# Hybrid decoder layer on one core: when the first attention loads may start, who stores two gate tiles, and how the planner counts transfers in flight

## The chip, the cores and the metric

The kernel runs on one core of a Trainium2 chip. The metric is device time in microseconds (us), as the median of several runs. Inputs and the output are float32 in device memory.

## The reference

One layer over 1040 tokens (16 learned tokens ahead of 1024) of width 1024. All four branches read the same projection z of the normalised input.

```python
h = rms_norm(h_res, pre_norm_g[i])
z = h @ w_in[i]                                    # 1024 -> 7328 columns
(pv, pg, cq, ckv, kr, mg, cu, cg, sbcx, sg, gl) = split_cols(z)
y_a = (pool_mixer(pv, ...) * silu(pg)) @ w_out_pool[i]
y_b = (mla_attention(cq, ckv, kr, ...) * silu(mg)) @ w_out_mla[i]      # 8 heads, causal
y_c = (conformer_conv(cu, ...) * silu(cg)) @ w_out_conf[i]
y_d = (short_conv(sbcx, ...) * silu(sg)) @ w_out_sc[i]
gts = sigmoid(gl + gate_bias[i])                   # four gates of 1024 channels
m = gts[0] * y_a + gts[1] * y_b + gts[2] * y_c + gts[3] * y_d
h_res = h_res + rms_norm(m @ w_o[i], post_norm_g[i])
```

In `mla_attention` a key has 64 columns of its own for each head and 32 rotary columns `k_rope` that all heads share.

## The kernel before

Float32 operands are split into a high and a low part and each product is made of three matmuls. The program has three stages, and each is planned and written out by itself.

**Projections.** Pairs of column blocks of `w_in` are loaded (`raw`), combined on VectorE (`ss`), split by ScalarE and GpSimd into operand tiles (`A`, `S`) and multiplied into the PSUM banks `pa` to `pd`. `out_gate` writes the gate tiles `th` to device memory: all by ScalarE's queue, but for the last pair (`g == 30`), which goes by GpSimd's queue. Work that needs earlier projections (convolution, norms, keys, queries, values, pool) runs beside this in four lanes. Keys go to `k` (64 rows for each head) and `kr` (32 rotary rows) in device memory.

**Attention.** The loop runs over 16 half-heads `(h, c)`, eight heads by two halves of 512 queries. `load_q` brings a query tile (`qt`, three buffers), `load_kv` a key tile and a value tile; there are two of each (`kt0`, `kt1`, `vt0`, `vt1`), used by even and by odd heads. The rotary rows of a key tile are loaded only once, since they are the same for all heads; `kt1` has them with their halves of 16 rows exchanged, as its queries do. `maxima` makes the scores once (`ps_s<-kt,qt`), takes masked maxima of the rows on VectorE (`mx`, with the mask `maskS` that GpSimd writes at the start of the stage), transposes the result (`ps_s<-ident,md`) and copies it into four further rows of `qt` (ScalarE, `qt<-ps_s`). `attend` makes scores (`ps_s<-qt,kt`), exponentials (`p`), a high part on ScalarE and a low part on GpSimd (`pt`), and the value products (`ps_o`). `head_out` divides (VectorE `op`), multiplies with the gate path (GpSimd `op<-op,smg`) and splits the result (`boM`). `refill` hands out 48 fills, six matmuls each (`ps_y<-bo,whl`, 288 in all): output projections of the three other branches, which the planner gives a low priority. Behind each fill VectorE multiplies with the gate (`th<-th,ps_y` or `m<-th,ps_y`) and, for the second and third branch, an addition follows (`m<-m,th`; for the third on VectorE).

**Output.** `ps_u<-boM,whl` is the attention's output projection; then come the product with `w_o`, the last norm and the stores.

**What sets the order.** `Plan.record` notes each operation with what it depends on and a priority. `Plan.flush` runs through estimated times, gives each engine the ready operation of highest priority that `fits`, and then writes all engines' instructions in that order. SyncE's queue (SP) issues nearly all transfers, in order, and blocks on the first one whose waits are not met. `fits` lets SP and ScalarE issue a transfer only while fewer than eight are thought to be in flight; `self.landed` holds their estimated landing times. `plan.behind()` makes what is recorded inside depend on the last matmul recorded so far.

Of the kernel before, what the change touches and what calls it, by code (L numbers as in the profile page):

```python
# [14 lines left out]

# [49 lines left out]
def f(ap):  # L65
    return ap.bitcast(F32)
# [127 lines left out]
class Plan:  # L194
# [139 lines left out]
    def flush(self):  # L334
# [26 lines left out]
        def slot(b, t):  # L361

            free = [sl for sl in b.group["slots"] if not sl["live"] and sl["after"] <= t]
            if free and (b.group["any"] or b.group["order"][b.group["next"]] is b):
                return min(free, key=lambda sl: (sl["after"], sl["i"]))

        def fits(o, t):

            if o["op"] == "dma_start" and o["eng"] != "POOL" and len(self.landed) >= 8 and self.landed[-8] > t:
                return False  # L370
            return all(slot(b, t) for b in o["bufs"] if not b.live and b.group)

        while events:
            t = events[0][0]
            while events and events[0][0] <= t:
                _, kind, i = heapq.heappop(events)
                if kind == 0:
                    o = self.ops[i]
                    bisect.insort(ready[o["eng"]], (o["prio"], o["i"]))
                elif kind == 2:  # L380
                    for b in self.ops[i]["bufs"]:
                        b.left -= 1
                        if b.left == 0 and b.group:
                            b.slot["live"], b.slot["after"] = None, t
            for e in self.free:
                if self.free[e] > t:
                    continue
                o = next((self.ops[i] for _, i in ready[e] if fits(self.ops[i], t)), None)
                if o is None:
                    if e == "PE" and self.idle and self.ops[self.idle[1]]["end"] is None:  # L390
                        order.append(self.idle[0])
                        self.free[e] = t + 160
                        heapq.heappush(events, (self.free[e], 1, 0))
                    continue
                ready[e].remove((o["prio"], o["i"]))
                for b in o["bufs"]:
                    if not b.live:
                        b.live = True
                        if b.group:
                            b.slot = slot(b, t)  # L400
                            b.slot["live"] = b
                            b.group["next"] += 1
                o["start"] = t
                if o["turns"]:
                    o["cost"] += max(0, self.port[{"DVE": "POOL", "POOL": "DVE"}[e]] - t) * 0.7
                    self.port[e] = t + o["cost"]
                self.free[e] = t + o["cost"]
                o["end"] = t + o["cost"] + self.WAKE[e]
                if o["op"] == "dma_start":
                    if self.pipe is None:  # L410
                        self.pipe = max((x["done"] for x in self.ops if x["op"] == "dma_start"
                                         and "done" in x and x["start"] <= t), default=0)
                    o["done"] = self.pipe = max(self.pipe, t) + o["bytes"]
                    land = self.pipe + o["bytes"] + 4500 + min(0, o["extra"])
                    o["end"] = land + max(0, o["extra"])
                    if o["eng"] != "POOL":
                        self.landed.append(land)
                    heapq.heappush(events, (land, 1, 0))
                for b in o["bufs"]:
                    b.last = max(b.last, o["end"])  # L420
                order.append(o)
                heapq.heappush(events, (self.free[e], 1, 0))
                heapq.heappush(events, (o["end"], 2, o["i"]))
                for u in o["users"]:
                    u["need"] -= 1
                    same = u["eng"] == e and o["op"] != "dma_start"
                    u["at"] = max(u["at"], self.free[e] if same else o["end"])
                    if not u["need"]:
                        heapq.heappush(events, (u["at"], 0, u["i"]))
# [8 lines left out]
def trunk_kernel(ctx, tc, a):  # L438
    nc = tc.nc
    plan = Plan(nc)  # L440
    PE, ACT, DVE, POOL, SP = (plan.engine(e) for e in ("PE", "ACT", "DVE", "POOL", "SP"))
# [7 lines left out]
    def ld(out, in_):  # L449
        SP.dma_start(f(out) if out.dtype == F32R else out, f(in_) if in_.dtype == F32R else in_)  # L450
# [38 lines left out]
    th_dram = [dram.tile([P, NT], F32, name=f"th{i}") for i in range(32)]  # L489
# [6 lines left out]
    kr_dram = dram.tile([32, 2, L], F32R, name="kr")  # L496
# [136 lines left out]
    def full(to, x, ps):  # L633

        if x is None:
            copy(to, ps)
        else:
            add(DVE, to, ps, x)

    def pairs_of_halves(n, each, store):  # L640

        z = {}

        def out(i, j, ps, x, tmp):
            first = i not in z
            if first:
                z[i] = up.tile([P, 2, n], F32, tag="z", bufs=2, name="z")
            m = ps.shape[0]
            each(i, z[i][:m, j], ps, x, tmp)
            if not first:  # L650
                store(i, z[i][:m])
        return out
# [11 lines left out]
    def row(t):  # L664
        return t.rearrange("p j n -> p (j n)")
# [16 lines left out]
    def out_gate(g):  # L682

        def each(i, to, ps, x, tmp):
            if x is not None:
                full(to, x, ps)
            ACT.activation(to, ps if x is None else to, AF.Tanh, scale=0.5,
                           bias=par[:, R_GB + g + i:R_GB + g + i + 1])
        return pairs_of_halves(512, each, lambda i, t: (POOL if g == 30 else ACT).dma_start(th_dram[g + i], row(t)))

# [587 lines left out]
    def load_q(h, c):  # L1280
        qt[h, c] = qk.tile([NA, 2, 512], F32R, tag="q", bufs=3, name="qt")
        ld(qt[h, c][:QK].rearrange("p s n -> p (s n)"), q_dram[c][h].rearrange("p s n -> p (s n)"))

    load_q(0, 0)
    kt = [qk.tile([NA, 2, L], F32R, name=f"kt{i}") for i in range(2)]
# [4 lines left out]
    def load_kv(h):  # L1290
        e, k_, v_ = h % 2, kt[h % 2], vt[h % 2]
        ld(k_[:64].rearrange("p s n -> p (s n)"), k_dram[h // 2][64 * e:64 * (e + 1)].rearrange("p s n -> p (s n)"))
        if h == 0:
            ld(k_[64:96], kr_dram)
        if h == 1:
            ld(k_[64:80], kr_dram[16:])
            ld(k_[80:96], kr_dram[:16])
        v = v_dram[h // 4][h % 4]
        ld(v_[:, 0:8].rearrange("p j c -> p (j c)"), v[:, 0:8].rearrange("p j c -> p (j c)"))
        ld(v_[:NM, 8], v[:NM, 8])  # L1300
# [95 lines left out]
    op, smg = {}, {}  # L1396
# [58 lines left out]
    def refill():  # L1455
        count["u"] += 1
        while count["f"] < min(48, 48 * count["u"] / (NUNIT - 2)):

            with plan.ahead(-400):
                next(fill, None)  # L1460
            count["f"] += 1
# [9 lines left out]
    def lead_to(i, n=0):  # L1471

        while lead["i"] <= min(i, len(seq) - 1) or lead["steps"] < n:
            if next(steps, "end") == "end":
                lead["steps"] = math.inf
            lead["steps"] += 1

    load_kv(0)
    load_q(*seq[1])
    lead_to(0)  # L1480
    units = 0
    for i, (h, c) in enumerate(seq):
        with plan.behind():
            if i + 2 < len(seq):
                load_q(*seq[i + 2])
            if c == 0 and h + 1 < H:
                load_kv(h + 1)
            if c == 0 and h % 2:
                smg[h] = at.tile([P, NT], F32, tag="smg", name="smg")
                ld(smg[h], z_dram[f"mg{h // 2}"])  # L1490
        for _ in attend(h, c):
            units += 1
            lead_to(-1, min(5 + units * 10 / 14, 5 * (i + 3)))
            refill()
        lead_to(i + 1)
        with plan.ahead(-300):
            if h == H - 1:
                head_out(h, c, sums_pe(h, c))
            elif c:
                for k, rb in enumerate(sums(h)):  # L1500
                    head_out(h, k, rb)
# [82 lines left out]
    for d in (0, 4, 1, 5, 2, 6, 3, 7):  # L1584
# [3 lines left out]
        for c in range(2):  # L1588
            t = th[:, 512 * c:512 * (c + 1)]
# [23 lines left out]
    def half(name, bufs=4):  # L1613
        return ep.tile([P, 512], F32, tag=name, bufs=bufs, name=name)
# [71 lines left out]
    for t in range(4):  # L1686

        parts = [slice(0, 512)] if t < 3 else [slice(0, 256), slice(256, 512)]
        g = half("g", 1) if t == 3 else a_[t]
# [45 lines left out]
```

## Time and profile before

| | us |
|---|---|
| median of 3 runs | 1018.12 (1017.72 to 1019.06) |
| the profiled execution | 1017.58 |
| its span in the profile | 1015.9 |
| TensorE busy in the span | 990.5 (98%) |
| GpSimd, VectorE, ScalarE busy | 685.6, 668.1, 455.4 |

The profiled execution has 1.68 us around its span and lies 0.54 us under the median. In the profile PE is TensorE's matmuls, PEld its weight loads, DVE VectorE, ACT ScalarE, POOL GpSimd, SPq the queue of SyncE. Names are the program's tile names; all recorded operations carry line 332, the helper that issues them, so they are told apart by tile. The first number of a row of the timeline is the start, the second the duration, and in brackets stands how long the engine was idle ahead of the row and what ended that. The stages meet at about 651 us (first attention score) and 883 us (first `ps_u`).

### The profile page before, as it was taken

To read this page: it belongs to the slowest core of one execution; us is meant where nothing else is said; L and a number is where in the kernel's file an instruction comes from. 1 tells how busy PE (TensorE), PEld (TensorE's weight loads), DVE (VectorE), ACT (ScalarE), POOL (GpSimd) and SP (SyncE) were. 2 spreads that over 40 slices of the span, in tenths; PEclk is the share of its full clock that TensorE was granted. 3 is DMA by queue.
4 is the path that set the end of the run, shared out by engine and by line. 5 is a ranking of instruction groups with operands and counts; after the bars stand their busy time and mean duration, and the time that the engine had idled before them with its cause. 6 is when DMAs were issued, how large, how long until landed. Compare 5 with 4: busy or idle time off the path is not lost.

```text
span 1015.9 us, 15303 instructions
## 1 busy us (share of the span) xinstructions
PE 990.5 (98%) x5139; PEld 831.7 (82%) x5139; DVE 668.1 (66%) x1106; ACT 455.4 (45%) x911; POOL 685.6 (67%) x640
## 2 busy tenths in 40 slices
PE   9999999999999999999999999989999999799996
PEld 9999898889888878887877888868887878588885
DVE  6754795997999499435455453255565675598747
ACT  7632234443354544444534444136556556224632
POOL 6767867766777666768776765125678876556956
PEclk9999999999999999999999999989999999899998
DMA  7278755679767856566656456877568671662634
GB/s 246 75 229 277 245 169 182 217 226 301 250 214 224 288 189 206 188 197 203 206 175 197 136 172 191 310 206 241 147 188 256 183 209 53 201 228 89 202 120 165
DMA packets 126302, 203.13 MB, mean 200 GB/s; under 512 B 19650, under 2 KB 79161, under 8 KB 124880
## 3 DMA queue, kind: packets, MB, share of 16 engines
q1 hardware_dynamic: 121600, 185.38, 58.2%
q10 hardware_dynamic: 4336, 15.73, 4.2%
q8 instruction: 40, 0.66, 0.3%
q0 software_dynamic: 288, 1.05, 0.3%
q14 instruction: 38, 0.31, 0.1%
HBM read 128.40 MB, written 73.72 MB: 199 GB/s over the span
## 4 chain that ended last, share of the span: by engine, by line
PE 91%; DVE 4%; issue 2%; DMA 1%; POOL 1%; ACT 1%; SPq 0%; DVEq 0%; POOLq 0%; ACTq 0%
PE ps_pa L332 16%; PE ps_pb L332 16%; PE ps_pc L332 15%; PE ps_o L332 10%; PE ps_y L332 8%; PE ps_s L332 7%; PE ps_pd L332 7%; PE ps_u L332 7%; PE ps_x L332 4%; DMA kt<-kr 1%; DVE x L332 1%; DVE a L332 1%; DMA x<-in_x_dram 0%; DVE ps_w L332 0%; DVE ss L332 0%
## 5 line engine op out<-in xcount | busy, mean ns | idle before, releaser
L332 PE MATMUL ps_pb<-T,S 128*128 128x512 f32 (+2 forms) x792 | 172.4, 362 | 0.8 <-DVE u L332 0.8
L332 PE MATMUL ps_pa<-B,A 128*128 128x512 f32 (+2 forms) x792 | 172.2, 362 | 0.0
L332 POOL TENSOR_TENSOR S<-ss,S 128x512 fp32r<-128x512 f32 x84 | 110.5, 1328 | 76.9 <-ACT S L332 76.7
L332 PEld LDWEIGHTS ps_pa<-B,A 128*128 128x128 f32 x792 | 134.6, 188 | 24.4 <-issue 0.5
L332 PEld LDWEIGHTS ps_pb<-T,S 128*128 128x128 f32 x792 | 133.8, 188 | 24.4 <-DVE u L332 1.2
L332 POOL TENSOR_TENSOR A<-raw,A 128x512 fp32r<-128x512 f32 x84 | 116.9, 1397 | 48.2 <-ACT A L332 44.7
L332 POOL TENSOR_TENSOR pt<-p,pt 128x512 fp32r<-128x512 f32 (+4 forms) x112 | 103.8, 955 | 43.5 <-PE ps_s L332 20.5
L332 ACT ACTIVATE S<-ss 128x512 fp32r<-128x512 f32 x84 | 50.8, 628 | 115.4 <-DVE ss L332 72.7
L332 PE MATMUL ps_y<-bo,whl 128*128 128x512 f32 x288 | 90.9, 418 | 6.2 <-DVE op L332 4.9
L332 DVE SCALAR_TENSOR_TENSOR ps_w<-conv,par,ps_w 128x512 f32<-128x512 f32 x116 | 87.2, 752 | 2.4
L332 PE MATMUL ps_pc<-B,S 128*128 128x512 f32 (+2 forms) x396 | 87.5, 364 | 0.5 <-DVE z L332 0.5
L332 PE MATMUL ps_pc<-T,S 128*128 128x512 f32 (+2 forms) x396 | 86.4, 363 | 0.4 <-DVE z L332 0.4
L332 PE MATMUL ps_pd<-T,A 128*128 128x512 f32 (+2 forms) x396 | 84.9, 361 | 0.0
L332 PEld LDWEIGHTS ps_pc<-T,S 128*128 128x128 f32 x396 | 67.1, 188 | 13.2 <-issue 1.0
L332 PEld LDWEIGHTS ps_pc<-B,S 128*128 128x128 f32 x396 | 66.8, 188 | 13.2 <-issue 1.0
L332 PE MATMUL ps_o<-pt,vt 128*128 128x512 f32 (+4 forms) x336 | 77.3, 336 | 0.1
L332 PEld LDWEIGHTS ps_pd<-T,A 128*128 128x128 f32 x396 | 66.9, 188 | 11.9
L332 PE MATMUL ps_s<-qt,kt 100*128 100x512 f32 (+4 forms) x336 | 69.4, 326 | 1.0 <-ACT qt L332 1.0
L332 ACT ACTIVATE A<-raw 128x512 fp32r<-128x512 f32 x84 | 52.7, 627 | 37.4 <-PE ps_pd L332 22.9
L332 ACT ACTIVATE p<-ps_s 128x512 f32<-128x512 f32 (+4 forms) x112 | 49.6, 443 | 38.3 <-DVE ps_s L332 15.6
L332 PEld LDWEIGHTS ps_y<-bo,whl 128*128 128x128 f32 x288 | 53.0, 197 | 14.7 <-DVE op L332 5.3
L332 PEld LDWEIGHTS ps_s<-qt,kt 100*128 100x128 f32 (+1 forms) x336 | 54.7, 176 | 12.5 <-ACT qt L332 1.1
(346 smaller groups left out, 1901.8 us busy)
## 6 DMA issues: line engine op xcount, KB each, us to landing
raw<-in_w_in_dram SPq DMA_DIRECT2D x56, 512.0 KB
th<-th SPq DMA_DIRECT2D x32, 512.0 KB
th<-z ACTq DMA_DIRECT2D x30, 512.0 KB
v<-vhl SPq DMA_DIRECT2D x16, 384.0 KB
qt<-q SPq DMA_DIRECT2D x16, 384.0 KB
vt<-v SPq DMA_DIRECT2D x8, 768.0 KB
bo<-bo SPq DMA_DIRECT2D x6, 1024.0 KB
kt<-k SPq DMA_DIRECT2D x8, 520.0 KB
```

Of the source, the lines that this page charges most:

```text
L332: getattr(self.handle[o["eng"]], o["op"])(*map(real, o["args"]), **{k: real(v) for k, v in o["kw"].items()})
```

## The change

Three edits of a few lines each.

1. *In flight by times.* `landed` keeps pairs of issue time and landing time, and `fits` counts how many of the last 40 transfers are in flight at the time in question. Before, it looked whether the eighth last transfer that was issued had landed.
2. *Stores by ScalarE.* The last two gate tiles are stored by ScalarE's queue as all others are.
3. *Loads of the first half-head.* In the first turn of the attention's loop the loads no longer stand behind the last recorded matmul. They are those of the third query tile, the second head's key tile and its value tile. The rotary rows of `kt1` are recorded with head 0's loads, and no longer with head 1's.

```diff
             if o["op"] == "dma_start" and o["eng"] != "POOL" and \
-                    len(self.landed) >= 8 and self.landed[-8] > t:
+                    sum(s <= t < e for s, e in self.landed[-40:]) >= 8:
                 return False
...
                     if o["eng"] != "POOL":
-                        self.landed.append(land)
+                        self.landed.append((t, land))
...
-        return pairs_of_halves(512, each, lambda i, t: (POOL if g == 30 else ACT).dma_start(th_dram[g + i], row(t)))
+        return pairs_of_halves(512, each, lambda i, t: ACT.dma_start(th_dram[g + i], row(t)))
...
         if h == 0:
             ld(k_[64:96], kr_dram)
-        if h == 1:
-            ld(k_[64:80], kr_dram[16:])
-            ld(k_[80:96], kr_dram[:16])
+            ld(kt[1][64:80], kr_dram[16:])
+            ld(kt[1][80:96], kr_dram[:16])
...
     for i, (h, c) in enumerate(seq):
-        with plan.behind():
+        with plan.behind() if i else nullcontext():
             if i + 2 < len(seq):
                 load_q(*seq[i + 2])
             if c == 0 and h + 1 < H:
                 load_kv(h + 1)
```

Since the planner sets the order, these edits move instructions on all engines, in the projections too. Three places follow.

The queue of SyncE where the stages meet, before: `kt_6728` and `vt_6737` are the tiles of head 0, and the ones of head 1 (`kt_6834`) come 23 rows after the first query tile.

```order
350 L332 DMA qt<-q_4509 96x1024
351 L332 DMA kt_6728<-k_2264 64x2080
352 L332 DMA kt_6728<-kr 32x2080
353 L332 DMA qt<-q_5597 96x1024
354 L332 DMA whl<-w_out_pool_710 128x512
355 L332 DMA whl<-w_out_pool_1013 128x512
356 L332 DMA vt_6737<-v_2870 128x1536
357 L332 DMA vt_6737<-v_2870 16x192
358 L332 DMA bo<-bo_5134 128x2048
359 L332 DMA bo<-bo_5646 128x2048
```

The same place after; `kt_6735` and `vt_6748` are the tiles of head 1.

```order
352 L332 DMA qt<-q_5693 96x1024
353 L332 DMA qt<-q_4567 96x1024
354 L332 DMA kt_6735<-kr 16x2080 x2
355 L332 DMA kt_6735<-k_2251 64x2080
356 L332 DMA whl<-w_out_pool_710 128x512
357 L332 DMA whl<-w_out_pool_981 128x512
358 L332 DMA vt_6745<-v_2906 128x1536
359 L332 DMA vt_6745<-v_2906 16x192
360 L332 DMA vt_6748<-v_2906 128x1536
361 L332 DMA vt_6748<-v_2906 16x192
362 L332 DMA bo<-bo_5233 128x2048
364 L332 DMA bo<-bo_5672 128x2048
```

Ahead of `whl` now stand four more transfers, and ahead of the two `bo` tiles another two.

TensorE at the start of attention, before:

```order
527 L332 MATMUL ps_y<-bo,whl 128x512 x4
528 L332 MATMUL ps_s<-kt_6728,qt 128x264
529 L332 MATMUL ps_y<-bo,whl 128x512 x44
530 L332 MATMUL ps_s<-kt_6728,qt 128x264
531 L332 MATMUL ps_s<-kt_6728,qt 128x328 x2
532 L332 MATMUL ps_s<-kt_6728,qt 128x392 x2
533 L332 MATMUL ps_s<-ident,md 4x128 x4
```

And after:

```order
539 L332 MATMUL ps_y<-bo,whl 128x512 x4
540 L332 MATMUL ps_s<-kt_6728,qt 128x264
541 L332 MATMUL ps_y<-bo,whl 128x512
542 L332 MATMUL ps_s<-kt_6728,qt 128x264
543 L332 MATMUL ps_y<-bo,whl 128x512 x3
544 L332 MATMUL ps_s<-kt_6728,qt 128x328
545 L332 MATMUL ps_y<-bo,whl 128x512 x2
546 L332 MATMUL ps_s<-kt_6728,qt 128x328
547 L332 MATMUL ps_y<-bo,whl 128x512
548 L332 MATMUL ps_s<-kt_6728,qt 128x392
549 L332 MATMUL ps_y<-bo,whl 128x512
551 L332 MATMUL ps_s<-ident,md 4x128 x4
```

Ahead of the first transposes of maxima (`ident,md`) stood 48 matmuls of fills; now there are 12, and the other 36 come later. GpSimd has its two `th` stores ahead of writing `maskS` before, and none after.

TensorE at the end of attention, before, in the last half-head; `ident,lcp` belongs to `head_out`:

```order
1154 L332 MATMUL ps_y<-bo,whl 128x512
1155 L332 MATMUL ps_y<-ident,lcp 64x128 x4
1156 L332 MATMUL ps_y<-bo,whl 128x512 x14
1157 L332 MATMUL ps_o<-pt,vt_6897 128x512
1158 L332 MATMUL ps_o<-pt,vt_6897 64x512
1159 L332 MATMUL ps_o<-pt,vt_6897 128x512
1160 L332 MATMUL ps_y<-bo,whl 128x512 x4
1161 L332 MATMUL ps_o<-pt,vt_6897 128x512
```

And after, from the middle of the last half-head to its end:

```order
1175 L332 MATMUL ps_y<-bo,whl 128x512 x5
1176 L332 MATMUL ps_o<-pt,vt_6748 128x512
...
1188 L332 MATMUL ps_o<-pt,vt_6748 128x16 x2
1189 L332 MATMUL ps_o<-pt,vt_6748 64x16
1190 L332 MATMUL ps_y<-ident,ol 128x64 x4
1191 L332 MATMUL ps_y<-bo,whl 128x512 x3
1192 L332 MATMUL ps_y<-ident,lcp 64x128 x4
1193 L332 MATMUL ps_y<-bo,whl 128x512 x19
```

Before, the fills ended with 14 and 4 between the value products of the last half-head, and none came behind the last value product. Now they stand in runs of at most five between the value products, and 22 follow the last one. On VectorE, 7 additions `m<-m,th` stood between the attention's last maxima and the output stage, and 12 do now.

More of the change, by code (lines that the diff above doesn't have):

```diff
@@ L13 @@
 import re
-from contextlib import ExitStack, contextmanager
+from contextlib import ExitStack, contextmanager, nullcontext
 import concourse.bass as bass
@@ L367, in fits @@
         def fits(o, t):
-            if o["op"] == "dma_start" and o["eng"] != "POOL" and len(self.landed) >= 8 and self.landed[-8] > t:
+            if o["op"] == "dma_start" and o["eng"] != "POOL" and sum(s <= t < e for s, e in self.landed[-40:]) >= 8:
                 return False
```

## The prediction

> **What bounds the kernel now.** I read the page first: busy shares and the chain that ended last. Of the chain, 91% is TensorE's matmuls.
>
> ```profile
> span 1015.9 us, 15303 instructions
> PE 990.5 (98%) x5139; PEld 831.7 (82%) x5139; DVE 668.1 (66%) x1106; ACT 455.4 (45%) x911; POOL 685.6 (67%) x640
> PEclk9999999999999999999999999989999999899998
> PE 91%; DVE 4%; issue 2%; DMA 1%; POOL 1%; ACT 1%; SPq 0%; DVEq 0%; POOLq 0%; ACTq 0%
> ```
>
> TensorE is idle for 1015.9 − 990.5 = 25.4 us, and its granted clock falls at two places within the run. As the matmuls' number does not change, the change can only move this idle time and the slow stretches. So I asked for TensorE's waits, longest in total first (us in total, times, longest), of which these are the larger and the ones used below.
>
> ```profile
> PE ps_y L332 <- DVE op L332: 4.9, 1, 4.9
> PE ps_s L332 <- DMA kt<-kr: 2.2, 1, 2.2
> ...
> PE ps_y L332 <- POOL lsq L332: 1.1, 1, 1.1
> ...
> PE ps_y L332 <- ACT ol L332: 0.7, 1, 0.7
> ...
> PE ps_y L332 <- DVE lcp L332: 0.3, 1, 0.3
> ```
>
> The rest of the idle time is waits of 1.4 us and less and the tail behind the last matmul, whose order on VectorE and ScalarE the change leaves as it is. The two waits at the top are the two places where the clock falls. Here are the stretches of 5 us around them: length, then busy time (and count) of PE, PEld, DVE, ACT, POOL, then granted clock, DMA share and GB/s.
>
> ```profile
> 670.00:675.00 5.00, 2.80 (x13) 2.21 (x12) 2.88 (x9) 1.33 (x6) 2.60 (x6) 0.89 0.96 253
> 675.00:680.00 5.00, 5.00 (x20) 3.98 (x20) 1.44 (x5) 0.60 (x1) 0.00 (x0) 0.50 0.44 119
> 680.00:685.00 5.00, 5.00 (x22) 4.09 (x22) 1.44 (x5) 2.95 (x6) 1.14 (x2) 0.92 0.40 111
> 870.00:875.00 5.00, 1.51 (x4) 1.22 (x5) 4.78 (x4) 0.44 (x2) 2.17 (x3) 0.69 1.03 372
> 875.00:880.00 5.00, 5.00 (x16) 3.75 (x15) 1.72 (x3) 0.39 (x2) 0.49 (x1) 0.63 0.93 353
> ```
>
> The reader sees that a wait costs twice: once while it lasts, and again for some microseconds behind it at half the clock, while TensorE counts as busy. The timeline of PE confirms it: three fills take 1.48 us in the slow stretch and 0.86 us later.
>
> ```profile
> 652.89 10.25 PE L332 MATMUL ps_y<-bo,whl 128*128 128x512 f32 x44
> 664.67 0.60 PE L332 MATMUL ps_s<-ident,md 128*4 128x128 f32 x4 [0.38 <-DVE mx L332]
> 666.03 1.89 PE L332 MATMUL ps_s<-qt,kt 100*128 100x512 f32 x9 [0.42 <-ACT qt L332]
> 673.73 0.31 PE L332 MATMUL ps_s<-kt,qt 96*128 96x144 f32 x1 [2.20 <-DMA kt<-kr]
> 677.83 1.48 PE L332 MATMUL ps_y<-bo,whl 128*128 128x512 f32 x3
> 695.57 0.86 PE L332 MATMUL ps_y<-bo,whl 128*128 128x512 f32 x3
> ```
>
> **Part 1: the rotary rows and the other early loads.** The rows that TensorE waited for were issued late; the queue of SP reads so, with two stretches of 5 us below (the last three numbers are clock, DMA share and GB/s):
>
> ```profile
> 618.62 0.30 SPq L332 DMA_DIRECT2D qt<-q  x1
> 631.48 1.02 SPq L332 DMA_DIRECT2D whl<-w_out_pool  x2
> 638.57 2.25 SPq L332 DMA_DIRECT2D bo<-bo  x2
> 664.54 1.04 SPq L332 DMA_DIRECT2D kt<-kr  x2
> 625.00:630.00 5.00, 1.00 0.04 13
> 640.00:645.00 5.00, 5.00 (x24) 1.00 0.90 344
> ```
>
> They were issued at 664.54 and waited for until 673.73. In the new order they stand directly behind the query tile of 618.62, where SP idles until 631.48 and DMA moves 13 GB/s (share 0.04) from 625 to 630. They should then land some 40 us before use.
> *Gain, the wait:* 2.20 us.
> *Gain, the clock:* from 675 to 685 TensorE was busy throughout and lost 5 × 0.50 + 5 × 0.08 = 2.9 us; of the 0.55 that 670 to 675 lost, part fell in the wait itself. The bounds are 2.9 and 3.45; I take 3.2.
> [...] The row of 0.50 directly behind the gap speaks for the cause, and so does the page's clock row: the shorter waits of the list have no dip behind them. [...]
>
> *What the loads are moved past.* Four issues (0.30 us for a query tile, 1.04 for two halves, about 0.5 for a key tile) go into SP's 12.5 us of idle time: nothing. Their data (by the shapes 96x1024, twice 16x2080 and 64x2080 in float32: 384 + 260 + 520 KB = 1.19 MB) takes 3.5 us at 344 GB/s, in a window that was empty: nothing. The value tile of head 1 (128x1536 and 16x192: 780 KB, 0.80 MB) now goes ahead of `bo`, so at 344 GB/s `bo` lands 2.3 us later. The fills' first use is at 651.85, 13 us behind the issue of `bo` at 638.57; the head value tile and both `bo` (128x2048 each; 0.80 + 2.10 MB together) take 8.4 us at that rate. Some 4 us of cover stay after adding 2.3: nothing. If the cover were gone, TensorE would wait at 652 by the excess, at most 2.3 us.
>
> **Part 2: the two stores by ScalarE.** They free GpSimd, which held everything behind them in its queue, the mask first:
>
> ```profile
> 650.61 0.77 POOL L332 DMA_DIRECT2D th<-z  x1 [16.38 <-ACT z L332]
> 653.39 0.54 POOL L332 DMA_DIRECT2D th<-z  x1 [2.01 <-ACT z L332]
> 653.91 0.55 POOL L332 MEMSET maskS<- 128x512 f32 x1
> 651.63 0.69 DVE L332 TENSOR_TENSOR z<-ps_pc,u 128x512 f32<-128x512 f32 x1 [2.09 <-PE ps_pc L332]
> 661.03 0.31 DVE L332 CUSTOM_DVE_ANT_0 ps_s<-ps_s,maskS 128x144 f32<-128x144 f32 x1
> 664.03 0.17 DVE L332 TENSOR_TENSOR md<-mr,negd 128x16 f32<-128x16 f32 x1
> 665.30 0.58 ACT L332 ACTIVATE qt<-ps_s 4x512 fp32r<-4x512 f32 x1 [12.23 <-PE ps_s L332]
> ```
>
> GpSimd had nothing to do for 16.38 us ahead of its first store; the masks now fall there. VectorE can begin the maxima when its last `z` is done, at 652.32, and not at 661.03. ScalarE, idle 12.23 us ahead of 665.30, issues two more transfers: nothing. TensorE used that time for 44 fills, 10.25 us, or 0.233 us each. So attention starts 36 × 0.233 = 8.4 us earlier and these fills come later: by itself this is worth nothing to an engine that is busy either way.
> Two waits change place with it. VectorE's chain from the first maximum to `md` took 664.20 − 661.03 = 3.2 us; from 652.32 it ends near 655.5, with the bank that the transposes need some 0.5 us after. TensorE has ten maxima scores (1.4 us) and 12 fills (2.8 us) from 651.43, so it arrives at 655.6. I expect waits as at 664.67 and 666.03 (0.38 and 0.42): difference nothing; bounds −0.8, if the fills cover them, and +1.5, if VectorE's bank comes a whole chain step later.
>
> **Part 3: the count in flight, and what the new order moves.** It moves instructions everywhere, without adding one. *Projections:* TensorE's waits there are no larger than 1.1 us each and add to about 3.4 without the start. The trace cannot show the new ones, so I take no change, with bounds −3.4 (all gone) and +3.4 (twice as many).
>
> *End of attention:* the longest wait of all is here.
>
> ```profile
> 866.91 5.82 DVE L332 TENSOR_TENSOR m<-m,th 128x512 f32<-128x512 f32 x1
> 867.99 4.18 POOL L332 TENSOR_TENSOR pt<-p,pt 128x512 fp32r<-128x512 f32 x4
> 873.49 3.78 PE L332 MATMUL ps_y<-bo,whl 128*128 128x512 f32 x8 [4.89 <-DVE op L332]
> 882.30 0.46 PE L332 MATMUL ps_y<-ident,ol 64*128 64x64 f32 x4 [0.69 <-ACT ol L332]
> L332 DVE TENSOR_TENSOR m<-m,th x32: 678/693/5818, 806.3 to 929.5; 128x512 f32<-128x512 f32 x32
> ```
>
> The last row gives this kind of addition its least, median and greatest duration: one of 32 took 5818 ns against a median of 693, over the four `pt` that GpSimd ran without a gap. The two banks of the fills stayed occupied, TensorE's queue stood at a fill for 4.89 us, and the clock lost 5 × 0.37 + 1.5 × 0.31 = 2.3 us behind it: 7.2 us in all.
> After, 22 fills (22 × 0.233 = 5.1 us) follow the last value product; they cover the two waits of 0.69 and 0.28 there: gain 1.0 us. The long wait I leave as it is. For it to shrink speaks that the fills lie in runs of at most five, not 14, between value products; for it to grow speaks that 12 additions of this kind, not 7, follow the last maxima on VectorE, with GpSimd's nine `pt` right behind its four instructions of `head_out`. Bounds: −7.2 (gone) and +7.2 (a second one).
> [...]
>
> **The sum.** −2.2 − 3.2 − 1.0 = −6.4 us. Against the profiled execution: 1017.58 − 6.4 = 1011.2. The median lies 0.54 above it, so 1018.12 − 6.4 = 1011.7 us.
>
> **The rivals.**
> *A, the long wait at the end goes too.* For it: the shorter runs, and attention that ends its GpSimd work 8.4 us earlier against TensorE's. Against: more additions there. 1011.7 − 7.2 = 1004.5 us.
> *B, the half clock stays.* [...] Against: waits of 0.8 to 1.1 us have no dip behind them. Only 2.2 + 1.0 come: 1014.9 us.
> *C, the new order gives it back in small waits.* In the projections or from `bo`: +3.4 + 2.3 against −6.4 leaves 1017.4 us. That the loads do not land early (SP blocked on a buffer ahead of them) gives about 1017 as well; the idle queue from 618.92 on speaks against it.
> *D, slower.* VectorE is shut out at the end more than once. One more event of 7.2 us gives 1018.9; from 8.4 us more the change is slower by over 0.2%, and two give 1026.1 us. For it: five more additions beside GpSimd's stream. Against: one event among 32.
>
> **How the numbers follow.** Forecast 0.47, A 0.18, B 0.12, C 0.12, D 0.11. A measurement tells about 0.2%, 2.0 us, from no change. Faster are the forecast, A, B and a part of C, less what the projections may take from B: 0.74. The rest of C and the milder D are the same: 0.15. Slower: 0.11. The forecast's own range is 1008 to 1015. The whole one goes from 1003.5 (A with a little help from the projections) to 1018.5 (C with all its bounds, D with hardly one event) and leaves out most of D and the far part of A.
>
> **What would show it.** Right: no wait on `kt<-kr` in TensorE's list, a granted clock of 1.00 from 655 to 690, `maskS` written before 651, the first maxima at 652, no wait of `ps_y` on ACT `ol`. A shows as a clock of 1.00 from 860 to 885. Wrong: a dip of the clock near 656 (B), a first `ps_y` that waits for DMA `bo` or waits in the projections of 2 us and more (C), additions `m<-m,th` over 3 us with `ps_y` waiting for VectorE (D).

## The result, and the profile after

The changed kernel takes 1032.91 us (median of 4 runs, 1031.88 to 1035.68) where the kernel before takes 1017.92 beside it: a ratio of 1.0155, interval 1.0126 to 1.0183. The prediction was 1011.7 with a range up to 1018.5, and it was wrong: 15 us are lost. One kernel's time spreads with the clock that its executions are granted: 25 executions of the kernel before, taken beside the first experiments, went from 1012.00 us at a mean granted clock of 0.996 to 1023.16 at 0.986. The page after, head, busy rows and clock row, and behind it the larger of TensorE's waits (us in total, times, longest):

```profile
span 1032.0 us, 15306 instructions
PE 993.5 (96%) x5139; PEld 834.5 (81%) x5139; DVE 667.6 (65%) x1106; ACT 455.3 (44%) x911; POOL 686.9 (67%) x638
PE   9999999999999999999999999399999989999996
PEclk9999999999999999999999999689999989999998
```

```profile
PE ps_y L332 <- DMA bo<-bo: 18.8, 2, 16.6
PE ps_s L332 <- DVE mx L332: 4.3, 2, 2.5
PE ps_s L332 <- ACT qt L332: 1.5, 3, 0.6
...
PE ps_y L332 <- DVE op L332: 0.6, 1, 0.6
```

The rows of before that spoke of `kt<-kr` (2.2), `op` (4.9), `ol` (0.7) and `lsq` (1.1) are gone or small. In their place stand a wait of 18.8 us for `bo` and two for `mx`. The first is the hole in the PE row (a 3 in the 26th slice). In stretches of 5 us (length, busy time and count of PE, PEld, DVE, ACT, POOL, then clock, DMA share, GB/s) the two places read:

```profile
645.00:650.00 5.00, 5.00 (x23) 4.09 (x22) 0.69 (x1) 1.41 (x2) 0.16 (x2) 1.00 0.00 0
650.00:655.00 5.00, 1.36 (x8) 0.91 (x6) 1.90 (x7) 0.72 (x1) 0.00 (x0) 0.91 0.57 213
655.00:660.00 5.00, 0.00 (x0) 0.00 (x0) 0.00 (x0) 0.00 (x0) 0.00 (x0) 0.50 0.99 258
660.00:665.00 5.00, 0.00 (x0) 0.00 (x0) 0.00 (x0) 0.00 (x0) 0.00 (x0) 0.50 1.00 401
665.00:670.00 5.00, 1.65 (x3) 0.83 (x3) 0.00 (x0) 0.00 (x0) 0.00 (x0) 0.50 1.01 415
670.00:675.00 5.00, 3.24 (x9) 2.77 (x10) 1.28 (x5) 0.00 (x0) 0.11 (x1) 0.50 0.95 366
675.00:680.00 5.00, 4.44 (x16) 3.21 (x16) 2.90 (x7) 0.58 (x1) 0.00 (x0) 0.70 0.17 58
...
790.00:795.00 5.00, 5.00 (x15) 3.96 (x16) 1.88 (x6) 3.70 (x7) 3.76 (x4) 0.66 1.00 282
845.00:850.00 5.00, 4.28 (x12) 3.15 (x13) 4.75 (x15) 2.12 (x5) 0.00 (x0) 0.53 0.51 200
850.00:855.00 5.00, 5.00 (x21) 4.08 (x21) 0.68 (x3) 4.70 (x9) 4.79 (x4) 0.79 0.30 105
```

From 645 to 650 no byte moves, and from 665 on DMA runs at 415 GB/s: the transfers were not slow, they were not sent. The queues of SyncE and ScalarE show who held them (a joined row, x2, reaches from the first issue to the end of the last):

```profile
638.68 13.93 SPq L332 DMA_DIRECT2D kt<-kr  x2
652.65 0.48 SPq L332 DMA_DIRECT2D kt<-k  x1
656.23 0.82 SPq L332 DMA_DIRECT2D whl<-w_out_pool  x2
657.15 1.78 SPq L332 DMA_DIRECT2D vt<-v  x4
659.03 0.38 SPq L332 DMA_DIRECT2D bo<-bo  x1
...
660.46 0.39 SPq L332 DMA_DIRECT2D bo<-bo  x1
...
649.68 0.33 ACTq L332 DMA_DIRECT2D th<-z  x1
652.46 0.33 ACTq L332 DMA_DIRECT2D th<-z  x1
...
SPq L332 <- DMA th<-z: 33.6, 4, 13.3
```

SyncE waits 33.6 us (between 610 and 665 us) for stores `th<-z`, which it does not read. The two stores that were moved to ScalarE account for 16.3 of it (13.3 ahead of the second `kt<-kr`, 3.0 ahead of `whl`), the two stores before them for the other 17.2. Before, the row of the same stretch was:

```profile
SPq L332 <- DMA th<-z: 4.9, 2, 3.6
```

Why it waits stands in the built program, as instructions that the build puts there: each of the 624 transfers of SyncE and ScalarE counts up one of eight completion counters, taken in turn over both queues, and before it goes out its queue waits until the transfer eight places back has landed (554 of them have just this wait written out). The waits of SyncE's rows at this place, after (`DMAHW0` is counter 0; `DVE` and `Pool` are waits for engines):

```
387 L332 DMA kt_6735<-kr 16x2080 [waits DMAHW7_49]
388 L332 DMA kt_6735<-kr 16x2080 [waits DMAHW0_49]
389 L332 DMA kt_6735<-k_2251 64x2080 [waits DMAHW1_49]
390 L332 DMA whl<-w_out_pool_710 128x512 [waits DMAHW2_49,DVE_49,Pool_49]
```

Counter 0 is that of the first store moved to ScalarE, counter 2 that of the second. The second `kt<-kr` goes out at about 652, 3 us behind the first store's issue, and `whl` at 656, behind the second's. GpSimd's two transfers in the program before count on counters of their own, `DMASW0` and `DMASW1`. The wait is in SyncE's queue, by the row of 13.93 us: everything behind it stood too, `kt<-k` until 652.65 and `whl` until 656.23.

By stage: from the first attention score (651.43 before, 650.78 after) to the first `ps_u` (883.42, 899.76) it is 232.0 us before and 249.0 after, 17.0 more. What lies ahead is 0.65 us shorter, the tail as long as it was (132.5 and 132.2). All comparisons below give this stretch as "the attention".

### The profile page after: what moved, and what is told of

Its sections match the earlier page's. It is cut to its first block, busy times and chain, and to the rows that moved or that the text cites. A ratio compares the mean times of both kernels' runs of the same rounds, so it can differ in the third digit from the quotient of the medians.

```text
span 1032.0 us, 15306 instructions
## 1 busy us (share of the span) xinstructions
PE 993.5 (96%) x5139; PEld 834.5 (81%) x5139; DVE 667.6 (65%) x1106; ACT 455.3 (44%) x911; POOL 686.9 (67%) x638
## 4 chain that ended last, share of the span: by engine, by line
PE 91%; DVE 5%; DMA 2%; issue 1%; ACT 1%; POOL 0%; SPq 0%; DVEq 0%; ACTq 0%; POOLq 0%
PE ps_pb L332 16%; PE ps_pa L332 16%; PE ps_pc L332 15%; PE ps_o L332 10%; PE ps_s L332 8%; PE ps_y L332 8%; PE ps_pd L332 7%; PE ps_u L332 7%; PE ps_x L332 4%; DMA bo<-bo 1%; DVE op L332 1%; DVE ps_w L332 1%; DMA kt<-k 1%; DVE x L332 1%; DVE a L332 1%
## 5 line engine op out<-in xcount | busy, mean ns | idle before, releaser
L332 POOL TENSOR_TENSOR S<-ss,S 128x512 fp32r<-128x512 f32 x84 | 113.5, 1363 | 72.7 <-ACT S L332 67.3
L332 POOL TENSOR_TENSOR A<-raw,A 128x512 fp32r<-128x512 f32 x84 | 115.3, 1381 | 44.8 <-ACT A L332 33.6
L332 PE MATMUL ps_y<-bo,whl 128*128 128x512 f32 x288 | 91.6, 417 | 19.4 <-DMA bo<-bo 18.8
L332 PE MATMUL ps_s<-qt,kt 100*128 100x512 f32 (+4 forms) x336 | 74.2, 341 | 1.6 <-ACT qt L332 1.5
L332 PEld LDWEIGHTS ps_s<-qt,kt 100*128 100x128 f32 (+1 forms) x336 | 57.3, 184 | 14.4 <-ACT qt L332 2.0
```

The source lines that it names most:

```text
L332: getattr(self.handle[o["eng"]], o["op"])(*map(real, o["args"]), **{k: real(v) for k, v in o["kw"].items()})
```

## Experiments

Each time stands with its ratio to the kernel before, run on the same chip.

**Only the counters of the two stores changed.** TensorE's, VectorE's and SyncE's orders stay word for word; the two stores leave by GpSimd's queue.

```diff
+        eng = "POOL" if o["op"] == "dma_start" and any(o["args"][0] is x for x in self.by_pool) else o["eng"]
...
+    plan.by_pool = [th_dram[30], th_dram[31]]
```

> The changed kernel with its whole order kept; only the last two gate stores go out from GpSimd's queue again, at the same places of the program. Theory 'counters': each transfer of SyncE's and ScalarE's queues takes one of eight completion counters, in the order of the program over both queues, and waits until the transfer eight before it has landed; the two stores that ScalarE issues at 649.68 and 652.46 us thereby hold up kt<-kr (to 652), whl (to 656) and both bo behind them. GpSimd's transfers have counters of their own, so here SyncE goes on at about 639, the 18.8 us wait of ps_y for bo and some 3.7 us of half clock behind it go, and the time is 1032.9 - 22.5 = 1010, or down to 1000 if the two waits on mx at 788 and 845 go as well. Theory 'traffic': the early loads (two megabytes ahead of bo) are what delays bo; they are all still there, so the wait stays at 10 us or more and the time above 1022. Theory 'order': the new plan is slow by itself; within 1 per cent of 1032.9.

1018.87 us, ratio 1.0014 (0.9989 to 1.0039), attention 233.1 in place of 249.0. `whl` leaves at 639.40 and `bo` at 642.38 and 644.64.

```profile
639.40 0.99 SPq L333 DMA_DIRECT2D whl<-w_out_pool  x2
...
642.38 0.37 SPq L333 DMA_DIRECT2D bo<-bo  x1
...
PE ps_s L333 <- DVE mx L333: 5.2, 3, 2.5
PE ps_y L333 <- DMA bo<-bo: 3.1, 1, 3.1
```

So nearly all of the loss hangs on the counters that the two stores took. The 15.9 us are what the trace lets one count: 18.8 idle and 3.8 at a lower clock (1.65 × 0.50 + 3.24 × 0.50 + 4.44 × 0.30) after, against 3.1 + 0.9 idle and 2.5 at a lower clock here. Of "traffic" a part is true too: 3.1 us of wait on `bo` are left, and the time stays above the 1010 expected. Even without the two late stores, then, the change gains nothing, where a ratio of 0.994 was predicted.

**One store each.** As above with `by_pool = [th_dram[31]]`, then with `[th_dram[30]]`.

> The changed kernel; only the first of the two gate stores that ScalarE issues (th31, at 649.68 us in the changed kernel) goes out from GpSimd's queue, the second (th30, 652.46) stays with ScalarE. Counters: the one store that is left lands at 656, and whl has its counter eight places on, so whl, the value tiles and both bo leave as late as in the changed kernel: 1033, wait of ps_y on bo 17 to 19 us. A theory by which it is the two stores' work or traffic that costs (half of it gone): about 1026.

> The other one: th31 stays with ScalarE, th30 goes out from GpSimd's queue. Counters: the store that is left lands at 652.2, and it is the key tile kt<-k that has its counter eight places on; from 652.7 all loads go out in a row, whl not 3 us later. bo leaves near 655.5 in place of 659, the wait on bo is about 15 us and the time about 1029. Half of the cost gone: about 1026, as for the other.

1030.31 us (1.0139, 1.0106 to 1.0172) and 1033.82 (1.0170, 1.0137 to 1.0204). SyncE's gap stands where the counter says, in the first kernel ahead of `whl`, in the second ahead of `kt<-k`:

```profile
637.29 0.49 SPq L333 DMA_DIRECT2D kt<-k  x1
654.68 0.82 SPq L333 DMA_DIRECT2D whl<-w_out_pool  x2
...
633.56 6.08 SPq L333 DMA_DIRECT2D kt<-kr  x2
653.01 0.49 SPq L333 DMA_DIRECT2D kt<-k  x1
```

In the first the wait on `bo` is 18.2 us, inside the 17 to 19 expected. One late store is enough; its traffic is not the cost, or half would have gone. The second kernel's gain of 3 to 4 us did not come: its `bo` left at 657.28 and 659.22 (655.5 expected), and the wait was 17.6 us. What held it is left open.

**The edits in pairs and alone.**

> Edits 1 and 3 without edit 2: the planner, too, puts the last two gate stores on GpSimd's queue, so GpSimd's masks and the first maxima stand behind them again. Counters: no wait on bo, no wait on kt<-kr, 1018 - 5.4 = 1012.6, range 1005 to 1016. Traffic: bo is late by the early loads, above 1020. Order: the count in flight alone moves the projections; 1018 +- 4.

1016.67 us, ratio 0.9993 (0.9967 to 1.0018): edits 1 and 3 without the stores lose nothing and gain less than expected (the range ended at 1016). `kt<-kr` is gone from the waits, but `bo`, at 640.74 and 642.73, is waited for 2.1 us, and the wait at the end stays 4.9.

> Edits 1 and 2 without edit 3: TensorE's, ScalarE's, VectorE's and GpSimd's orders are those of the changed kernel, word for word; only ten rows of SyncE differ, the early loads stand behind bo again. Counters: the first value tile has the counter of the store that lands at 652, the first bo that of the store that lands at 656, so bo is issued at 656 in place of 659 and only 0.8 MB go ahead of it; the wait of ps_y on bo shrinks from 18.8 to about 10 us, and the time is about 1024 (1021 to 1029). Traffic: without the early loads no wait on bo, 1010 to 1016.

1030.50 us, ratio 1.0119 (1.0070 to 1.0169), wait on `bo` 14.2 us. Against "traffic" this decides: with no early load at all the loss is there. The value tile left at 652.63 and `bo` at 658.83, not 656; SyncE stands at the counters, but `bo` was 3 us later than I reckoned, and so the time misses its range. Why the second store's counter came free only then is not shown.

> Edit 3 alone: on the kernel before, only SyncE's order changes (18 rows) and nine rows of TensorE. GpSimd stores the last two gate tiles, so no store stands in the counters of the early loads. Counters: the prediction's part 1 comes as it was written, 1018.0 - 5.4 = 1012.6 (1010 to 1016). Traffic: bo comes late, above 1019.

1012.37 us, ratio 0.9962 (0.9938 to 0.9987), attention 225.6, 6.4 us less than before. Edit 3 by itself does what part 1 of the prediction said: no wait on `kt<-kr`, none on `bo`, and the clock there (third number from the end) is full. By its ratio the gain is 3.9 us, with an interval from 1.3 to 6.3 that holds the 5.4 of part 1; that 1012.37 lies so near 1012.6 is luck in part, since the kernel before ran at 1015.92 beside it.

```profile
670.00:675.00 5.00, 5.00 (x33) 4.27 (x32) 4.17 (x15) 2.07 (x7) 2.75 (x6) 1.00 0.57 184
675.00:680.00 5.00, 5.00 (x24) 4.07 (x23) 1.44 (x5) 3.30 (x6) 1.49 (x3) 1.00 0.46 146
```

> Edit 1 alone, the count in flight by times; stores and loads as in the kernel before. Counters and shut out together: no late store stands in the counters of bo, so no wait on bo; the wait on kt<-kr (2.2 us and the half clock behind it) and the long wait at the end (4.9 us and its dip) both stay, and the projections differ by no more than the 1.1 us wait on lsq: within 0.3 per cent of the kernel before. If the new count by itself slows the projections, as the third rival of the prediction had it: up to 3.4 us more.

1013.79 us, ratio 0.9973 (0.9946 to 0.9999), with the two waits of 2.2 and 4.9 us as before: the new count alone costs nothing.

> Edit 2 alone. Here the planner too knows the two stores as ScalarE's, and it puts head 1's key and value tiles ahead of bo. Counters: th31 has the counter of the query tile behind the first value tile, th30 that of kt<-kr; everything behind them, bo too, leaves after 656, so TensorE waits about 15 us for bo and the time is 1026 to 1034. If it takes the early loads of edit 3 together with the stores to lose time: 1018 or less.

1015.70 us, ratio 1.0004 (0.9988 to 1.0020). This broke the theory as I had put it. SyncE is held just as long, and still nobody waits for `bo`, since TensorE's first fill comes at 672:

```profile
652.65 0.30 SPq L332 DMA_DIRECT2D qt<-q  x1
...
659.37 0.84 SPq L332 DMA_DIRECT2D bo<-bo  x2
...
672.17 0.64 PE L332 MATMUL ps_y<-bo,whl 128*128 128x512 f32 x2
```

In the changed kernel the first fill stands at 651, ahead of the second score. I put the difference down to the planner's rule, though edit 3 is absent here too; the next run has it. The old rule held a transfer back until the eighth last had landed, which is the rule of the counters in another form; by its own estimates `bo` would go out at 659.45 with edit 2 alone. With edit 1 in its place it reckoned with 635.6, and the chip sent it at 659.03. By this account the wait on `bo` takes the stores and the new count together: the stores close the queue, and the count hides that from the planner, which writes TensorE's order.

> Edits 2 and 3 with the planner's old rule (a transfer goes out only when the eighth before it has landed). Edit 2 alone showed SyncE held until 657 as in the changed kernel (bo at 659.37), and yet no wait on bo, since TensorE's first fill came at 672 there. Theory 'blind planner': the old rule is the counters' rule, so the planner knew bo to be late (it reckoned with 659.5) and put scores where the changed kernel, which reckoned with 635.6, puts fills. Then edits 2 and 3 with the old rule show SyncE held until 656 again, no wait on bo over 1 us, and 1008 to 1017. Rival: early loads and stores by ScalarE lose time together, whatever the planner reckons: a wait on bo of 15 us and 1026 or more.

1027.29 us, ratio 1.0122 (1.0087 to 1.0158): half right. No wait on `bo`, though SyncE stood at the value tile until 655; but the time missed its range by 10 us. The attention is 12.9 us longer than with edit 2 alone, and two places account for some 12: the start (650 to 680), where TensorE with few fills to do is idle for 4.4 us and loses 6.0 to the clock (1.7 and 3.2 there in the other), and one wait of 4.6 us that ends at 763 with 2.2 lost behind it. That one is the mechanism of the prediction's rival D, on a tiny instruction:

```profile
755.12 2.58 POOL L332 TENSOR_TENSOR boM<-op,boM 128x512 fp32r<-128x512 f32 x2
756.97 5.43 DVE L332 TENSOR_TENSOR md<-mr,negd 128x16 f32<-128x16 f32 x1
757.64 4.73 POOL L332 TENSOR_TENSOR pt<-p,pt 128x512 fp32r<-128x512 f32 x4
...
L332 DVE TENSOR_TENSOR md<-mr,negd x16: 174/176/5435, 656.3 to 863.6; 128x16 f32<-128x16 f32 x16
```

So that a planner which knows the counters avoids the wait on `bo` is seen twice (edit 2, edits 2 and 3) against twice with the wait (edits 1 and 2, all three); what it is worth in time is not, since each plan also shifts where VectorE is shut out.

**Where VectorE is shut out.** In the changed kernel the two waits on `mx` follow these rows:

```profile
783.15 3.76 POOL L332 TENSOR_TENSOR m<-m,th 128x512 f32<-128x512 f32 x3
784.00 4.07 DVE L332 TENSOR_TENSOR op<-ol,rb 64x512 f32<-64x512 f32 x2
...
839.67 1.28 POOL L332 TENSOR_TENSOR m<-m,th 128x512 f32<-128x512 f32 x1
839.99 4.62 DVE L332 TENSOR_TENSOR op<-ol,rb 64x512 f32<-64x512 f32 x2
840.96 2.50 POOL L332 TENSOR_TENSOR m<-m,th 128x512 f32<-128x512 f32 x2
```

Two `op<-ol,rb`, of 0.68 us each by the median, end 4.07 and 4.62 us after the first began, beside GpSimd's additions that follow each other without a gap; the reduction `mr<-mx` stands behind them. The test moves those additions:

```diff
                         add(POOL if bi == 1 else DVE, m_[c][d], m_[c][d], t)
+                        if bi == 1 and (d, c) in ((1, 0), (1, 1), (2, 0), (6, 1), (7, 0), (7, 1)):
+                            plan.other[plan.ops[-1]["i"]] = "DVE"
```

> The changed kernel with both stores back on GpSimd's queue (1018.9 us, three waits on mx of 5.2 us in all), and besides six of the sixteen additions m<-m,th that GpSimd does for the second branch moved to VectorE, at the same places of the program: those that ran without a gap beside the two long op<-ol,rb (4.1 and 4.6 us in place of 0.68). Theory 'shut out': these runs of GpSimd kept VectorE from its additions with two operands, mx came late, and TensorE's clock fell; without them no op<-ol,rb is over 2 us, the two longer waits on mx go with the clock behind them, about 10 us in all: 1009 to 1012. Rival: VectorE is late because it has too much to do there; four more microseconds of work for it then give no gain or a loss, 1018 to 1022.

1011.29 us, ratio 0.9952 (0.9935 to 0.9969); the longest `op<-ol,rb` is 1.77 us (4.01 without the edit), the longest wait on `mx` 0.8, and the attention is 7.6 us shorter than with the two stores moved alone, although VectorE has six additions more; about 10 were counted. The same at the end of the attention, on edit 3 alone; VectorE's order there, before and after the move:

```diff
 SCALAR_TENSOR_TENSOR th<-th,ps_y 128x512
-TENSOR_TENSOR m<-m,th 128x512
 TENSOR_TENSOR op<-ol,ps_y 64x512
 SCALAR_TENSOR_TENSOR th<-th,ps_y 128x512
-TENSOR_TENSOR m<-m,th 128x512
 SCALAR_TENSOR_TENSOR th<-th,ps_y 128x512
-TENSOR_TENSOR m<-m,th 128x512
 SCALAR_TENSOR_TENSOR th<-th,ps_y 128x512
+TENSOR_TENSOR m<-m,th 128x512 x3
```

> Edit 3 alone (1012.4 us), and three additions m<-m,th of VectorE near the end of the attention moved three to six places back in its order, behind the last multiplication with a gate; nothing else moves. In edit 3 alone the first of them takes 5.83 us beside GpSimd's six instructions and TensorE waits 4.9 us. Shut out: the multiplications, with an operand in PSUM, are not kept waiting and free the banks; the wait of ps_y on op and the dip of the clock behind it go, 7.2 us: 1005. Rival: what sets the end there is GpSimd's pt, which ps_o needs anyway; then a part comes back as a wait of ps_o on pt, 1008 to 1012.

1006.13 us, ratio 0.9902 (0.9879 to 0.9925), the best of all kernels here. The attention falls from 225.6 to 218.2 us, by 7.3 where 7.2 was counted; by the ratios the whole gains 6.1. In this profile the projections are 2.6 us longer than with edit 3 alone, with TensorE's order the same: around a wait of 1.1 us on `lsq` that both have, the clock is 0.93 from 350 to 375 here; the trace of before, with the same wait, has 1.00 there. All of TensorE's waits between 655 and 905 us are now these, and the longest addition is down from 5.83 to 1.45 us:

```profile
PE ps_s L332 <- ACT qt L332: 1.0, 2, 0.6
PE ps_y L332 <- DVE th L332: 1.0, 2, 0.6
PE ps_y L332 <- ACT ol L332: 0.7, 1, 0.7
PE ps_s L332 <- DVE z L332: 0.4, 1, 0.4
PE ps_y L332 <- DVE lcp L332: 0.3, 1, 0.3
...
L332 DVE TENSOR_TENSOR m<-m,th x32: 677/693/1453, 803.0 to 918.4; 128x512 f32<-128x512 f32 x32
```

## Why the prediction was wrong

*Part 2, the stores: ScalarE "issues two more transfers: nothing".* This step failed. I priced the stores where they are issued and not in the counters that they take, so that SyncE, and `whl` and `bo` with it, waited for them to land. It cost 15.9 us by the run without; the wait on `bo` and the lower clock behind it are 22.6 us in the trace, against 6.5 at the same place in that run. The part's other half held: the masks were written from 635.20 and the maxima began with the attention.

*Part 1, "what the loads are moved past: nothing".* Also wrong, for the same reason. SyncE's idle time from 618.92 to 631.48 was free only for transfers whose counter was. With edit 3 alone the three `kt<-kr` left by 621.67, but `kt<-k` at 637.50; with edits 1 and 3 the two for head 1 took from 621.30 to 632.62 and `kt<-k` left at 637.17, together held 15.2 us by the `th<-z` that ScalarE issued at 629.70 and 632.48. So the key and value tiles left just ahead of `bo` and not in the idle time, and the 4 us of cover did not hold (by the part's own figures 13.3 − 8.4 − 2.3 leaves 2.5, not 4): 2.1 us of wait with edits 1 and 3, 3.1 in the changed order. The bound "at most 2.3" for it came from data alone.

*Part 1, the gain: −2.2 − 3.2.* Right. The wait is gone in the changed kernel too, and edit 3 alone, which changes little else, shortened the attention by 6.4 us. In finer stretches the trace of before has the clock at 0.50 from 673.94 to 680.77, which is 3.4 us. With edit 3 alone, without the gap, the clock is 1.00 from 670 to 680: the half clock went with the gap of 2.20 us. One premise of the working does not hold beyond the trace of before, though: that waits of 0.8 to 1.1 us have no dip behind them. With the three additions moved, the clock is 0.93 from 350 to 375, where the wait of 1.1 us on `lsq` is the only wait; before, with the same wait, it is 1.00.

*Part 3.* The projections: no change, as taken. The end: the waits there fell from 5.9 to 1.1 us, more than the −1.0 taken, so rival A came true at its place. The sum did not price it, so for the prediction it is luck. The wait of 4.9 us is gone in every kernel planned with edit 2 and there in every one planned without it, but for the one that moves the three additions; which move of the new order did it was not tried. Rival D's mechanism came true at two other places, 784 and 840, where nobody looked. By the trace the two cost 10.0 us (4.3 for `mx`, 1.0 for `qt` behind it, 4.7 of clock), by the run that removes them 7.6. So the shut-out gave 7.1 us at the end and took 7.6 to 10.0 elsewhere.

*The sum, by the trace:* −5.4 for the rows, +22.6 for `bo`, +10.0 for the two shut-outs, −7.1 at the end, −2.1 for small waits (`th`, `mx`, `qt` of before) make +18.0; measured 17.0. Without the loss on `bo` the sum would be −4.6, near the −6.4 forecast, but only because the end's gain, which was not forecast, offsets much of the shut-outs; and the run without the late stores kept 6.5 us of the loss on `bo`, so that its attention is 1.1 us longer than before.

*Rival C* named "SP blocked on a buffer ahead" and gave it 1017: the right suspicion, too cheaply priced, since it took the late loads to forfeit the gain and not to carry `whl` and `bo` with them. The row that speaks for more was in the trace of before: the 4.9 us that SyncE waits for `th<-z`.

## What to carry to other kernels

An idle queue is not a free queue: ask what its next transfer waits for. Where transfers take eight completion counters in turn, as in this program, count them as one counts buffers, so that a store that ends late is never eight places ahead of a load that is needed soon; here it cost 15.9 us. A planner's rule that looks crude may be the model of such a limit; before it is replaced, compare its estimates with the issue times of the trace. Where GpSimd runs several instructions in a row, look at VectorE's additions with two operands in SBUF beside them: in the kernel before, one of 32 `m<-m,th` took 5.82 us (median 0.69), and none of 32 `th<-th,ps_y`, with an operand in PSUM, over 0.69. Put them behind what frees a PSUM bank, not ahead of it: that shortened the attention by 7.3 us here.

## What was not expected of the hardware

With edits 2 and 3, a run of GpSimd instructions held VectorE off to the end of the run: 5.43 us for a 128x16 operation of 0.17 us, beside the end of `boM` and four `pt` of 1.18 us each. Mostly one instruction is all: in the changed kernel 16 VectorE instructions with two operands in SBUF (`m<-m,th`, `op<-ol,rb`, `md<-mr,negd`) began while GpSimd ran an instruction with another right behind it, and 14 went in after that one; the two at 784 and 840 were held to the end of the run. At the end of the attention, where rival D was expected, additions went in between nine `pt`:

```profile
879.94 10.93 POOL L332 TENSOR_TENSOR pt<-p,pt 128x512 fp32r<-128x512 f32 x9
882.85 1.08 DVE L332 TENSOR_TENSOR m<-m,th 128x512 f32<-128x512 f32 x1
```

What decides between the two was not found; the longest division takes 4.01 us in four profiles that keep the changed kernel's order of VectorE and its additions on GpSimd, and the fifth (edits 1 and 2) has the same two waits on `mx`, 4.3 us together. Nor did the clock fall only behind a gap like that of 2.20 us: with edit 2 alone three waits of 0.37, 0.38 and 0.42 us within 4.1 us (652.07 to 656.16) stand ahead of and in a stretch at 0.62:

```profile
655.00:660.00 5.00, 4.58 (x18) 3.79 (x15) 2.72 (x10) 2.27 (x5) 0.40 (x1) 0.62 1.08 294
```

Whether their sum or their density does it was not tried.
